# One product of the gate's seven issued behind two products of what follows, in the feed-forward part of a hybrid attention block

## The chip, the cores and the metric

The kernel runs on one core of one Trainium2 chip. The metric is the device time of one execution in microseconds (us). "Products" below are groups of matmuls on TensorE (PE); the other engines are VectorE (DVE), ScalarE (ACT), GpSimd (POOL) and the engine that issues most transfers, SyncE (SP).

## The reference

The block takes x of 2048 tokens by 1024 columns in f32. It adds to x what two kinds of attention give, and then a gated feed-forward layer:

```python
h = x
u = rms_norm(h, norm1_w)
p = u @ w_in                      # columns: diff q | k | v | sb q | k | v
yA = diff_attention(...)          # 4 heads, two softmax maps each
yB = stick_breaking_attention(...)  # 8 heads
h = h + concat(yA, yB) @ w_out
v = rms_norm(h, norm2_w)
h = h + (silu(v @ w_gate) * (v @ w_up)) @ w_down      # 2816 columns between
```

Only the last line, the feed-forward layer, is touched by the change.

## The kernel before, in words

**Precision.** Every large factor is held as two f16 parts, hi and lo, and a product of two such factors is three matmuls: hi by hi, lo by hi, hi by lo.

**Tiling.** The feed-forward layer runs in two halves of 1024 tokens. A half goes through 11 groups of 256 of the 2816 columns, so there are 22 steps, numbered 0 to 10 (first half) and 11 to 21 (second half). A step has a `gate` part and an `up` part; the `down` products of the groups are collected and done for two groups at once ("two units"), after the gates of steps 2, 4, 6, 8, 10, 11, 13, 15, 17 and 19, and once more at the end.

**Seven products.** A gate or an up is a 2 by 2 block product done with seven products in place of eight (`quad`). Each product (`product`, L1027 to L1031) is 12 matmuls of 128x512. They come in this order, each followed by its eviction from PSUM: the first, `pa` (ACT copy, L1043); `p6` (DVE add, L1047); `p7` (DVE add, L1052); `pd` (DVE add, L1057, which gives the finished block c22); a second term added into `pa`; `p4` (DVE subtract, L1067); and the seventh, which is added into the bank of `pd` (DVE add, L1071). So the seventh can't begin before L1057 has read that bank. It multiplies the seventh weight block by the token block `X[3]`. A finished block of the gate goes through SiLU on ACT (L1083, `cg` tiles). A finished block of the up is multiplied with its gate block on DVE (L1103), mixed (L98), cut into hi on ACT (L1097) and lo (L98) and kept as `act`, the input of `down`. `down` (L1131 to L1187) runs over four groups of tokens, j = 0 to 3, with seven products each (L1138); DVE accumulates them into `hs` (L1144).

**The weights' chains.** In the first half the f32 weights of the coming group are scaled and cut while the products of this group run. `load_ffn` (L921 to L1025) is a generator that does this for the gate's weights, the up's and the down's, one after the other. For each: a transfer into `stages`; a square on ACT into `sq` (L954); for gate and up a sum down the columns on PE into a bank `fsc` (L963, eight 128x256 matmuls) and its maximum on DVE (L964), for down a transposing product on PE (L183) and a maximum on DVE (L184); six or seven small DVE instructions that make the scale (L135 to L205); the mixes of blocks on POOL (L98) into `sq` and `sx`; hi parts on ACT (L216) and lo parts on DVE (L221) into the f16 tile `wg`, `wu` or `wd`; and a transfer of that tile to memory, since the second half reads it from there (L944) instead. There is one `sq`: the square of the next weights (L954) waits until the last lo part has been read out of it (L221).

**What sets the order.** The program text is a list of tiles and instructions with their dependences; a scheduler with its own estimates of durations orders each engine's instructions. Within the text the generator is advanced by hooks: `quad` calls `at(1)` to `at(7)` after its products, the last behind the seventh product, and each call issues one step of a chain. The matmuls of a chain, L963 and L183, stand inside `behind()` (L899), an order edge: they may not be placed ahead of the last matmul that `product` (or `down`'s `prod`) had issued by then, which `front[0]` remembers. It is an edge of order alone and waits for no result.

**The second half's tokens.** In steps 0 and 1 the second half's token blocks are built as well (`build_x`, L1189 to L1221, with transposes on PE, L1213, into `xtr`).

Of the kernel before, what the change touches and what calls it, by code (L numbers as in the profile page):

```python
# [16 lines left out]
ALU = mybir.AluOpType  # L17
# [23 lines left out]
CU = 3  # L41
# [18 lines left out]
def block(tc, a, out):  # L60
# [3 lines left out]
    with top:  # L64
# [64 lines left out]
        half = c1(2, "half")  # L129
# [744 lines left out]
        with ExitStack() as ph2:  # L874
# [151 lines left out]
            def product(ps_, wv, wo, X, xo, start, stop):  # L1026
                q = 0  # L1027
                for kt in range(4):
                    for xi, wi in ((0, 0), (1, 0), (0, 1)):
                        front[0] = PE.matmul(ps_[:].rearrange("p (t n) -> p t n", n=P), lhsT=wv[:, wo, wi, 128 * kt : 128 * kt + 128], rhs=X[xo][:, :, xi, kt, :], start=start and q == 0, stop=stop and q == 11, skip_group_check=not start).ins  # L1030
                        q += 1  # L1031

            def quad(wv, X, tag, bufs, c11, hooks):
                def at(n):
                    hooks(n)

                def cst():
                    return fp.tile([P, 512], F32, tag=tag, bufs=bufs, name=nm(tag))

                pa = pst("pa")  # L1040
                product(pa, wv, 0, X, 0, True, True)
                u2 = cst()
                ACT.copy(u2[:], pa[:])  # L1043
                at(1)
                p6 = pst("pm")
                product(p6, wv, 4, X, 4, True, True)
                DVE.tensor_tensor(u2[:], p6[:], u2[:], ALU.add)  # L1047
                at(2)
                p7 = pst("pm")
                product(p7, wv, 6, X, 5, True, True)  # L1050
                u3 = cst()
                DVE.tensor_tensor(u3[:], p7[:], u2[:], ALU.add)  # L1052
                at(3)
                pd = pst("pd")
                product(pd, wv, 2, X, 2, True, True)
                c22 = cst()
                DVE.tensor_tensor(c22[:], pd[:], u3[:], ALU.add)  # L1057
# [12 lines left out]
                product(pd, wv, 5, X, 3, False, True)  # L1070
                DVE.tensor_tensor(u2[:], u2[:], pd[:], ALU.add)  # L1071
                c11(0, 1, u2)
                at(7)

            def gate(W, X, hooks):
                sg = {}

                def on_gate(f, t, c):
                    if (f, t) == (0, 0):
                        s = fp.tile([P, 512], F32, tag="cg", bufs=5, name=nm("cg"))  # L1080
                    else:
                        s = c
                    ACT.activation(s[:], c[:], AF.Silu, scale=W["kg"][:])  # L1083
                    sg[f, t] = s

                quad(W["g"], X, "cg", 5, on_gate, hooks)
                note("A", 2000)
                return sg

            def up(W, X, sg, hooks, final=False):  # L1090
                if final:
                    act = stages[:].rearrange("p b n -> p (b n)").bitcast(F16)[:, :7168].rearrange("p (o s n) -> p o s n", o=7, s=2)
                else:
                    act = fp.tile([P, 7, 2, 512], F16, tag="act", bufs=2, name=nm("act"))

                def put(o, src):
                    ACT.copy(act[:, o, 0], src)  # L1097
                    note("A", 500)
                    tt(act[:, o, 1], src, act[:, o, 0], ALU.subtract, 512, LE)

                def on_up(f, t, c):
                    s = sg[f, t][:]
                    DVE.scalar_tensor_tensor(s, c[:], W["F"][:], s, op0=ALU.mult, op1=ALU.mult)  # L1103
                    if (f, t) != (0, 1):
                        put({(0, 0): 0, (1, 0): 1, (1, 1): 3}[f, t], s)
                        return
                    a11, a12, a21, a22 = (sg[k][:] for k in ((0, 0), (1, 0), (0, 1), (1, 1)))
                    s3 = fp.tile([P, 512], F32, tag="cu", bufs=CU, name=nm("cu"))
                    tt(s3[:], a11, a21, ALU.subtract, 512, SE)
                    tt(a21, a21, a22, ALU.add, 512, SE)  # L1110
                    put(2, a21)
                    tt(a11, a21, a11, ALU.subtract, 512, SE)
                    tt(a12, a12, a11, ALU.subtract, 512, SE)
                    put(6, a12)
                    put(4, a11)
                    put(5, s3[:])

                quad(W["u"], X, "cu", CU, on_up, hooks)
                note("D", 2440)
                return act  # L1120

# [6 lines left out]
                    SP.dma_start(h[q][:], hd[8 * half + 2 * j + q])  # L1128
                return h

            def down(half, units, hs, last, hook=None):  # L1131
                kd = units[-1][0]["kd"]
                nu = len(units)

                def prod(po, ao, wo, j, start=True):
                    for u, (W, act) in enumerate(units):
                        for q, (xi, wi) in enumerate(((0, 0), (0, 1), (1, 0))):
                            front[0] = PE.matmul(po[:], lhsT=act[:, ao, xi, 128 * j : 128 * j + 128], rhs=W["d"][:, wo, wi, :], start=start and u == 0 and q == 0, stop=u == nu - 1 and q == 2, skip_group_check=not start).ins  # L1138
# [12 lines left out]
                ahead = [first(j) for j in range(4)] if nu == 3 else []  # L1151
                for j in range(4):
                    if j == 2 and hook is not None:
                        hook()
                    if j + 1 < 4:
                        hs.append(load_hs(half, j + 1, nu == 3, last))
                    h0, h1 = hs[j]
                    c11, c12, c21, c22 = h0[:, :512], h0[:, 512:], h1[:, :512], h1[:, 512:]
                    note("D", 3600)
                    note("A", 500)  # L1160
                    ae = "D" if last and j == 3 else AE
                    pa = ahead.pop(0) if ahead else first(j)
                    u2 = ust()
                    ACT.mul(u2[:], pa[:], kd[:])
                    pb = pst("pd")
                    prod(pb, 4, 4, j)
                    acc(u2[:], pb, u2[:])
                    pc = pst("pd")
                    prod(pc, 5, 6, j)
                    u3 = ust()  # L1170
                    acc(u3[:], pc, u2[:])
                    tt(c12, c12, u2[:], ALU.add, 512, ae)
                    pd = pst("pd")
                    prod(pd, 2, 2, j)
                    prod(pa, 1, 1, j, False)
                    acc(c22, pd, c22)
                    prod(pd, 6, 3, j, False)
                    acc(c11, pa, c11)
                    pe = pst("pd")
                    prod(pe, 3, 5, j)  # L1180
                    acc(c12, pd, c12)
                    acc(c21, pe, c21)
                    tt(c21, c21, u3[:], ALU.add, 512, ae)
                    tt(c22, c22, u3[:], ALU.add, 512, ae)
                    for q in range(2):
                        t = 8 * half + 2 * j + q
                        SP.dma_start(out[t * P : (t + 1) * P, :] if last else hd[t], hs[j][q][:])  # L1187
# [31 lines left out]
            W = {}  # L1219
# [37 lines left out]
            for i, (half, fg) in enumerate(steps):  # L1257
# [48 lines left out]
                        go("u")  # L1306
                    row(7 + s)

                sg = gate(W, X, in_gate)
                if not more:  # L1310
                    load_now(half, fg, "d", W)
                if due:
                    down(dh, units, hs, dh != half, lambda: go("g"))
                    units = []
                act = up(W, X, sg, in_up, not more)
                if more and steps[i + 1][0] == 1:
                    go("u", 9)
                units.append((W, act))
# [27 lines left out]
```

## Time and profile before

| | |
|---|---|
| median of three runs | 2679.39 us (2678.89 to 2686.21) |
| the profiled execution's own time | 2682.59 us |
| its span in the profile | 2680.8 us |
| its mean granted TensorE clock | 0.984 |
| feed-forward part of the span, by the first and last of its instructions | about 1427 to 2681 us |
| steps 0 to 10 (first half) | about 1427 to 2060 us |

The profile's times count from the start of the span. In a row of the timeline the first number is the start of a group of like instructions, the second how long they took, then come the engine, the line of the kernel, what is written and what is read, the tile's shape, how many there were, and in brackets how long the engine was idle just before and whose end released it. In an answer on waits the three numbers are the summed idle time, how often it came, and the longest. "PEclk" is the TensorE clock that was granted, 1.00 being full speed. Step 0 begins at 1427 us, the downs of step 6 at about 1777, those of step 10 at about 2002.

### The profile page before, as it was taken

The page shows a single profiled execution, that of the slowest core. Times are in us where ns is not written, and L with a number is a line of the kernel's source. Part 1 is how long each engine was busy: PE and PEld are TensorE (multiplying, and loading weights), DVE is VectorE, ACT ScalarE, POOL GpSimd, SP SyncE. Part 2 cuts the span into 40 slices and gives each one's busy share as a digit, 9 for nine tenths or more (in the row PEclk, how much of TensorE's full clock was granted, in tenths as well). Part 3 has the DMA queues.
Part 4 walks back from the last instruction along what each step waited for, and adds up shares of the span by engine and source line. Part 5 has one row for each costly group of instructions (what it writes and reads, how often), then busy time and mean ns, then how long its engine had stood idle before and what let it go on. Part 6 is the DMA issues. An engine that isn't in the chain of part 4 may idle for free. (4 is left out here: it accounts for less than half of the span.)

```text
span 2680.8 us, 50579 instructions
## 1 busy us (share of the span) xinstructions
PE 2492.4 (93%) x19628; PEld 1498.6 (56%) x19628; DVE 1932.7 (72%) x3711; ACT 1347.0 (50%) x2487; POOL 1489.1 (56%) x1098
## 2 busy tenths in 40 slices
PE   6998989888988989889989899999999999999999
PEld 4655656577776776557775344444444444444444
DVE  6898969898989989877766868777685544444434
ACT  4665656567978878665644535344352112111121
POOL 2578667667767766546764656565564232322323
PEclk9999999999999999999999899999999999999999
DMA  6777697767998979987897574665649743635532
GB/s 222 213 162 181 146 200 168 179 143 184 193 179 179 185 160 209 210 191 217 218 285 282 208 250 178 255 226 202 245 183 346 293 177 143 233 141 186 195 111 95
DMA packets 619585, 534.41 MB, mean 199 GB/s; under 512 B 480640, under 2 KB 548224, under 8 KB 609104
## 3 DMA queue, kind: packets, MB, share of 16 engines
q1 hardware_dynamic: 617520, 529.09, 69.9%
q8 instruction: 154, 2.52, 0.4%
q0 software_dynamic: 512, 1.36, 0.2%
q14 instruction: 87, 0.71, 0.1%
q10 hardware_dynamic: 1312, 0.72, 0.1%
HBM read 261.08 MB, written 147.32 MB: 152 GB/s over the span
## 5 line engine op out<-in xcount | busy, mean ns | idle before, releaser
L98 POOL TENSOR_TENSOR s<-z,s 128x1024 f16<-128x1024 f32 (+7 forms) x288 | 472.0, 1647 | 142.5 <-ACT s L89 109.8
L507 PE MATMUL sc<-kT,qT 128*128 128x512 f16 (+3 forms) x1520 | 382.0, 353 | 53.3 <-DVE z L623 19.3
L622 DVE TENSOR_TENSOR_SCAN z<-z,sc 128x512 f32<-128x512 f32 (+3 forms) x320 | 352.8, 1112 | 58.6 <-ACT sc L620 38.0
L1138 PE MATMUL pd<-wd,act 128*128 128x512 f16 x1764 | 390.9, 379 | 1.2 <-DVE cg L1071 1.2
L326 PE MATMUL pj<-w,xt 128*128 128x384 f16 x1920 | 352.2, 331 | 18.8 <-ACT xt L683 6.9
L1030 PEld LDWEIGHTS <-wg 128*128 128x128 f16 x1848 | 182.0, 99 | 230.2 <-issue 16.4
L518 PE MATMUL yp<-v,aT 128*128 128x64 f16 (+1 forms) x4896 | 269.8, 204 | 41.6 <-DMA aT<-s 40.2
L518 PEld LDWEIGHTS <-aT 128*128 128x128 f16 x4896 | 237.5, 99 | 120.4 <-DMA aT<-s 52.5
L1030 PEld LDWEIGHTS <-wu 128*128 128x128 f16 x1848 | 180.7, 98 | 218.0 <-issue 2.6
L98 POOL TENSOR_TENSOR act<-cg,act 128x512 f16<-128x512 f32 x112 | 148.5, 1337 | 262.9 <-ACT act L1097 150.8
L1138 PEld LDWEIGHTS <-act 128*128 128x128 f16 x1764 | 172.8, 98 | 209.4 <-issue 2.8
L326 PEld LDWEIGHTS <-xt 128*128 128x128 f16 x1920 | 187.3, 99 | 147.5 <-issue 21.4
L89 ACT CAST s<-z 128x128 f16<-128x128 f32 (+7 forms) x215 | 173.1, 809 | 134.1 <-DMA aT<-s 40.5
L98 POOL TENSOR_TENSOR hs<-hs,cu 128x512 f32<-128x512 f32 x99 | 130.9, 1328 | 171.3 <-DVE hs L1144 70.8
L619 ACT ACTIVATE z<-sc,c 128x512 f32<-128x512 f32 (+3 forms) x320 | 210.7, 663 | 25.6 <-PE sc L507 11.7
L1097 ACT CAST act<-cg 128x512 f16<-128x512 f32 x126 | 77.3, 616 | 238.4 <-DVE cg L1103 162.7
L507 PEld LDWEIGHTS <-qT 128*128 128x128 f16 x1520 | 128.4, 99 | 121.0 <-DVE z L623 23.0
L832 PE MATMUL po<-wo,mt 128*128 128x256 f16 x1536 | 180.7, 277 | 13.9 <-DVE xf L835 8.4
L1030 PE MATMUL pm<-X,wu 128*128 128x512 f16 x792 | 180.4, 379 | 1.3 <-DVE wu L221 1.3
L1030 PE MATMUL pm<-X,wg 128*128 128x512 f16 x792 | 181.3, 382 | 0.0
L342 PE MATMUL pj<-xt,w 128*128 128x128 f16 x2304 | 175.0, 220 | 6.7 <-DVE v L364 5.7
L1144 DVE SCALAR_TENSOR_TENSOR hs<-pd,c,hs 128x512 f32<-128x512 f32 x136 | 99.0, 747 | 109.6 <-PE pd L1138 83.1
(266 smaller groups left out, 4737.6 us busy)
## 6 DMA issues: line engine op xcount, KB each, us to landing
xt<-xs SPq DMA_DIRECT2D x112, 512.0 KB, 4.3
hs<-hd SPq DMA_DIRECT2D x68, 512.0 KB, 4.5
hd<-hs SPq DMA_DIRECT2D x56, 512.0 KB, 4.7
split<-wg SPq DMA_DIRECT2D x11, 1792.0 KB, 7.8
split<-wu SPq DMA_DIRECT2D x11, 1792.0 KB, 6.7
split<-wd SPq DMA_DIRECT2D x11, 1792.0 KB, 7.2
wg<-split SPq DMA_DIRECT2D x11, 1792.0 KB, 7.3
wd<-split SPq DMA_DIRECT2D x11, 1792.0 KB, 12.2
```

Of the source, the lines that this page charges most:

```text
L89: ACT.copy(dst, src)
L98: (DVE if e == "D" else POOL).tensor_tensor(dst, a_, b_, op)
L326: PE.matmul(pj[:, :384], lhsT=xv[:, xi, kt, :], rhs=G["w"][:, wi, kt, :], start=n == 0, stop=n == 23)
L342: PE.matmul(o, lhsT=x_ if c == 2 else w_, rhs=w_ if c == 2 else x_, start=n == 0, stop=n == 23)
L507: last = PE.matmul(sc[:, : 128 * w].rearrange("p (t n) -> p t n", n=P), lhsT=G["q"][i // 4][:, a_, i % 4, :], rhs=G["k"][q][:, b_, 0:w, :] ...
L518: PE.matmul(yp[:, y0 : y0 + wd], lhsT=aT[:, a_, :], rhs=v[:, v_ : v_ + wd], start=start and j == 0 and q == 0, stop=stop and j == nb - 1 a ...
L619: ACT.activation(om[:, lo:hi], sc[:, :w], AF.Sigmoid, scale=G["nkz"][:])
L622: DVE.tensor_tensor_scan(ov, ov, sc[:, :w], om[:, hi : hi + 1], op0=ALU.mult, op1=ALU.bypass)
L832: PE.matmul(po[:, sl], lhsT=mt[:, kt, P * xi : P * xi + P], rhs=wos[2 * h + n][wi][:, kt, :], start=q == 0, stop=q == 23)
L1030: front[0] = PE.matmul(ps_[:].rearrange("p (t n) -> p t n", n=P), lhsT=wv[:, wo, wi, 128 * kt : 128 * kt + 128], rhs=X[xo][:, :, xi, kt, : ...
L1138: front[0] = PE.matmul(po[:], lhsT=act[:, ao, xi, 128 * j : 128 * j + 128], rhs=W["d"][:, wo, wi, :], start=start and u == 0 and q == 0, s ...
L1144: DVE.scalar_tensor_tensor(dst, po[:], kd[:], src, op0=ALU.mult, op1=ALU.add)
```

## The change

`gate` no longer issues its seventh product. `quad` puts that product, its eviction (L1071), the SiLU behind it and the last hook `at(7)` into a function `seventh`. Where a `down` follows the gate (steps 2, 4, 6, 8, 10, 11, 13, ...), it is called there for j = 0 behind the second product and its accumulation; where `up` follows, it is called behind up's second product (`p6`) and its add. The 12 matmuls of the moved product stand inside `behind()`, so they may not be placed ahead of the last matmul of that second product. Up's own seventh product stays where it was. Nothing else of the text changes; the number of matmuls, transfers and evictions is the same.

```diff
-            def quad(wv, X, tag, bufs, c11, hooks):
+            def quad(wv, X, tag, bufs, c11, hooks, before=None, late=False):
...
                 product(p6, wv, 4, X, 4, True, True)
                 DVE.tensor_tensor(u2[:], p6[:], u2[:], ALU.add)
+                if before is not None:
+                    before()
                 at(2)
...
                 at(6)
-                product(pd, wv, 5, X, 3, False, True)
-                DVE.tensor_tensor(u2[:], u2[:], pd[:], ALU.add)
-                c11(0, 1, u2)
-                at(7)
+
+                def seventh():
+                    with behind() if late else nullcontext():
+                        product(pd, wv, 5, X, 3, False, True)
+                    DVE.tensor_tensor(u2[:], u2[:], pd[:], ALU.add)
+                    c11(0, 1, u2)
+                    at(7)
+
+                if not late:
+                    seventh()
+                return seventh
...
-                quad(W["g"], X, "cg", 5, on_gate, hooks)
+                seventh = quad(W["g"], X, "cg", 5, on_gate, hooks, None, True)
...
-            def up(W, X, sg, hooks, final=False):
+            def up(W, X, sg, hooks, final=False, before=None):
...
-                quad(W["u"], X, "cu", CU, on_up, hooks)
+                quad(W["u"], X, "cu", CU, on_up, hooks, before)
...
                     acc(u2[:], pb, u2[:])
+                    if before is not None and j == 0:
+                        before()
...
-                sg = gate(W, X, in_gate)
+                sg, seventh = gate(W, X, in_gate)
...
-                    down(dh, units, hs, dh != half, lambda: go("g"))
-                    units = []
-                act = up(W, X, sg, in_up, not more)
+                    down(dh, units, hs, dh != half, lambda: go("g"), seventh)
+                    units, seventh = [], None
+                act = up(W, X, sg, in_up, not more, seventh)
```

Line numbers below L1047 shift in the changed kernel: L1057 becomes L1059, L1067 L1069, the seventh's eviction L1071 becomes L1076, L1103 becomes L1112, L1138 becomes L1147, L1213 becomes L1224.

The scheduler answers with an order that differs in more places than the edge names. Three of them follow. Tile numbers such as `_24811` are the compiler's and differ a little between the two kernels; of a product's 12 matmuls the first row stands for all.

**First place: PE in step 1**, from the end of the gate to the start of the up. `wg` is the gate's weights, `wu` the up's; `pd_22827<-X_22367` is the gate's seventh product, `fsc` the columns' sum of the next gate's weights. Before:

```order
L1030 MATMUL pm_22865<-X_22148,wg_22541 128x512
...
L1030 MATMUL pd_22827<-X_22367,wg_22541 128x512
...
L1213 MATMUL xtr_22929<-id_63,bx_22377 128x128 x4
L1030 MATMUL pm_22986<-X_21893,wu_22776 128x512
...
L963 MATMUL fsc_22900<-sq_22883,ones 128x256
...
L1030 MATMUL pa_22942<-X_21889,wu_22776 128x512
...
L1030 MATMUL pm_22966<-X_21891,wu_22776 128x512
```

In the changed kernel, same place:

```order
L1030 MATMUL pm_22865<-X_22148,wg_22543 128x512
...
L1030 MATMUL pa_22886<-X_21889,wu_22776 128x512
...
L1224 MATMUL xtr_22925<-id_63,bx_22376 128x128 x4
L1030 MATMUL pm_22986<-X_21893,wu_22776 128x512
...
L963 MATMUL fsc_22902<-sq_22883,ones 128x256
...
L1030 MATMUL pm_22943<-X_21891,wu_22776 128x512
...
L1030 MATMUL pd_22827<-X_22367,wg_22543 128x512
```

The first product of the up (`pa`) has taken the place of the gate's seventh, which now stands behind four of the up's products; the up's `p7` (`pm_22986`) and the columns' sum stay where they were.

**Second place: PE at the end of step 5's up and the gate of step 6.** `pd_24898<-X_22367` is the up's own seventh, `fsc_24917` the transposing product of the down weights' chain (L183), `pm_24948` the up's `p4`, `pd_25081<-X_22367` the gate's seventh. Before:

```order
L1030 MATMUL pa_24830<-X_22144,wu_24700 128x512
...
L183 MATMUL fsc_24917<-id_63,m_24894 128x128
L1030 MATMUL pm_24948<-X_22148,wu_24700 128x512
...
L1030 MATMUL pd_24898<-X_22367,wu_24700 128x512
...
L963 MATMUL fsc_25043<-sq_25005,ones 128x256
...
L1030 MATMUL pm_25119<-X_22148,wg_24811 128x512
...
L1030 MATMUL pd_25081<-X_22367,wg_24811 128x512
...
L1138 MATMUL pd_25184<-wd_24578,act_24497 128x512
```

In the changed kernel:

```order
L1030 MATMUL pa_24798<-X_22144,wu_24700 128x512
...
L1030 MATMUL pd_24898<-X_22367,wu_24700 128x512
...
L183 MATMUL fsc_24917<-id_63,m_24894 128x128
L1030 MATMUL pm_24948<-X_22148,wu_24700 128x512
...
L963 MATMUL fsc_25043<-sq_25005,ones 128x256
...
L1030 MATMUL pm_25119<-X_22148,wg_24813 128x512
...
L1147 MATMUL pd_25143<-wd_24578,act_24497 128x512
...
L1030 MATMUL pd_25081<-X_22367,wg_24813 128x512
```

The up's seventh has moved ahead of the down weights' L183, which now stands 16 matmuls later; the columns' sum L963 of the next weights stands behind the same number of matmuls as before; and the gate's seventh stands behind 27 matmuls of the down. The end of step 9 and the gate of step 10 show the same two moves. In the downs of steps 4 and 8 the columns' sum of the next gate's weights stands 20 and 18 matmuls earlier than before.

**Third place: DVE at the same point**, from the chain's maximum (L184) to the lo part of `wd` that is read out of `sq` (`sq_24893`), behind which the next square may begin. Before:

```order
L184 TENSOR_REDUCE m_24918<-fsc_24917 128x1
L201 TENSOR_SCALAR m_24918<-m_24918 128x1
...
L135 TENSOR_SCALAR c_24971<-c_24971,c_24533 128x1
L1067 TENSOR_TENSOR cu_24880<-cu_24880,pm_24948 128x512
L221 SCALAR_TENSOR_TENSOR wd_24916<-stages,c_24892,wd_24916 128x2x512
L1103 SCALAR_TENSOR_TENSOR cg_24731<-cu_24880,c_24534,cg_24731 128x512
L221 SCALAR_TENSOR_TENSOR wd_24916<-stages,c_24892,wd_24916 128x2x512
L221 SCALAR_TENSOR_TENSOR wd_24916<-sq_24893,c_24892,wd_24916 128x2x512
```

In the changed kernel, with most of the small instructions of the scale and two evictions left out:

```order
L184 TENSOR_REDUCE m_24918<-fsc_24917 128x1
L98 TENSOR_TENSOR cu_24989<-cg_24769,cg_24682 128x512
...
L98 TENSOR_TENSOR cg_24682<-cg_24682,cg_24752 128x512
...
L98 TENSOR_TENSOR cg_24769<-cg_24682,cg_24769 128x512
...
L135 TENSOR_SCALAR c_24971<-c_24971,c_24533 128x1
L1047 TENSOR_TENSOR cg_25024<-pm_25028,cg_25024 128x512
L98 TENSOR_TENSOR act_24797<-cg_24731,act_24797 128x512
L221 SCALAR_TENSOR_TENSOR wd_24916<-stages,c_24892,wd_24916 128x2x512
L98 TENSOR_TENSOR cg_24731<-cg_24731,cg_24769 128x512
L221 SCALAR_TENSOR_TENSOR wd_24916<-stages,c_24892,wd_24916 128x2x512
L221 SCALAR_TENSOR_TENSOR wd_24916<-sq_24893,c_24892,wd_24916 128x2x512
```

Three mixes of the up (L98) now stand between the maximum and the scale, and another L98, a lo part of `act` and the gate's L1047 between the scale and the last lo part; before, they stood behind it.

More of the change, by code (lines that the diff above doesn't have):

```diff
@@ L1084, in on_gate @@
                     sg[f, t] = s
-                quad(W["g"], X, "cg", 5, on_gate, hooks)
+                seventh = quad(W["g"], X, "cg", 5, on_gate, hooks, None, True)
                 note("A", 2000)
-                return sg
-            def up(W, X, sg, hooks, final=False):
+                return sg, seventh
+            def up(W, X, sg, hooks, final=False, before=None):
                 if final:
@@ L1129, in load_hs, with down @@
                 return h
-            def down(half, units, hs, last, hook=None):
+            def down(half, units, hs, last, hook=None, before=None):
                 kd = units[-1][0]["kd"]
```

## The prediction

> **What bounds the kernel now.** I first read the totals of the feed-forward part by stretches of time, then who keeps TensorE waiting there, then the timeline around each of those waits. Stretches; a group in brackets is the number of instructions:
>
> ```profile
> core 0: us, PE busy (x) PEld busy (x) DVE busy (x) ACT busy (x) POOL busy (x), PEclk, DMA share, GB/s
> 1427.00:2110.00 683.00, 662.54 (x3138) 309.77 (x3137) 500.93 (x749) 298.88 (x362) 379.63 (x267) 0.99 0.65 240
> 2110.00:2619.00 509.00, 509.00 (x2360) 230.72 (x2359) 212.92 (x276) 92.47 (x147) 150.42 (x119) 1.00 0.46 170
> 1469.00:1494.00 25.00, 19.53 (x89) 8.79 (x87) 24.51 (x30) 11.78 (x18) 16.60 (x12) 0.89 0.41 136
> 1494.00:1503.00 9.00, 9.00 (x52) 5.35 (x51) 2.93 (x12) 6.36 (x9) 4.71 (x4) 0.93 0.68 268
> 1503.00:1532.00 29.00, 24.38 (x114) 11.07 (x112) 27.95 (x33) 15.13 (x20) 17.57 (x10) 1.00 0.66 222
> ```
>
> In the second half (second row) PE is busy 509.00 of 509.00 us. What an order of the same matmuls can win lies in the first half, where PE idles 683.00 - 662.54 = 20.46 us. What ended those waits (summed us, how often, longest):
>
> ```profile
> PE pd L1030 <- DVE cg L1057: 8.9, 3, 5.5
> PE fsc L963 <- ACT sq L954: 5.9, 1, 5.9
> ...
> PE pm L1030 <- DVE wu L221: 1.3, 2, 0.7
> ```
>
> The first row is the wait that the change goes at: the gate's seventh product wants the bank of `pd`, and L1057 must have read it. It occurs three times in 22 gates, 8.9 us in all. The second row is the next weights' square, late for its columns' sum.
>
> **Steps 0 to 2: about -5 us.** The timeline of the waits there:
>
> ```profile
> 1443.88 2.76 PE L1030 MATMUL pd<-X,wg 128*128 128x512 f16 x12 [0.96 <-DMA X<-xcd]
> 1491.13 4.76 PE L1030 MATMUL pd<-X,wg 128*128 128x512 f16 x12 [5.47 <-DVE cg L1057]
> 1529.73 2.17 DVE L221 SCALAR_TENSOR_TENSOR wd<-sq,c,wd 128x1024 f16<-128x1024 f32 x1
> 1531.94 1.91 ACT L954 ACTIVATE sq<-stages 128x2048 bf16<-128x2048 f32 x1 [3.11 <-DVE wd L221]
> 1533.90 1.87 PE L963 MATMUL fsc<-sq,ones 128*128 128x256 bf16 x8 [5.88 <-ACT sq L954]
> 1535.56 7.34 PE L1030 MATMUL pm<-X,wg 128*128 128x512 f16 x24
> 1547.98 1.46 PE L1138 MATMUL pd<-wd,act 128*128 128x512 f16 x6 [1.19 <-DVE cg L1071]
> ```
>
> and two of DVE's own waits between 1470 and 1545 us:
>
> ```profile
> DVE cg L1052 <- PE pm L1030: 3.2, 1, 3.2
> ...
> DVE cg L1071 <- PE pd L1030: 1.2, 1, 1.2
> ```
>
> Step 0's gate waits 0.96 us for `X[3]`, the last token block to arrive; the block is needed two products later now, so this goes. In step 1 the seventh waits 5.47 us, and its 12 matmuls then take 4.76 us in place of 2.75: 2.0 us of lost clock. In the changed order the up's products stand there instead. But that up's third product reads the last lo part of `wu`, which DVE writes at about 1490, so most of the gap comes back in front of it: I count 3.4 us returned. Further back stands DVE. In the stretches above it is busy 24.51 of 25 us and 27.95 of 29, and rests only in between, at 1494 to 1503, when it has to wait for PE. So what PE wins in step 1 it waits out again in front of the columns' sum at 1533.90, except as far as DVE's rest of 9.00 - 2.93 = 6.07 us can be used. Of that rest 3.2 + 1.2 = 4.4 us are waits for PE's products, and they shrink if PE comes earlier; the remainder is not. I take the 4.4 and half of the wait of 1.19 at 1547.98: -5. Bounds: 0, if DVE's queue comes no earlier at all, and -8 (6.07, 1.19 and the 0.96 of step 0, 8.2).
>
> **Steps 4 and 8: about +1.8 us.** When `down` follows, the columns' sum inside it stands about 18 matmuls nearer to the columns' sum that its chain begins with:
>
> ```profile
> 1654.09 1.04 PE L963 MATMUL fsc<-sq,ones 128*128 128x256 bf16 x8
> 1664.74 1.91 ACT L954 ACTIVATE sq<-stages 128x2048 bf16<-128x2048 f32 x1 [1.12 <-DVE wu L221]
> 1668.99 1.04 PE L963 MATMUL fsc<-sq,ones 128*128 128x256 bf16 x8
> 1765.27 5.34 PE L1030 MATMUL pm<-X,wg 128*128 128x512 f16 x24
> 1895.84 1.91 ACT L954 ACTIVATE sq<-stages 128x2048 bf16<-128x2048 f32 x1 [1.10 <-DVE wu L221]
> 1900.29 1.04 PE L963 MATMUL fsc<-sq,ones 128*128 128x256 bf16 x8
> ```
>
> One matmul more in a sequence costs 0.216 us: 24 take 5.34 us where 12 take 2.76 (first row of steps 0 to 2), about 2.59 for each further twelve. 18 of them are 3.9 us. The square ends at 1664.74 + 1.91 = 1666.65, in step 8 at 1897.75. The covers are 1668.99 - 1666.65 = 2.3 us and 1900.29 - 1897.75 = 2.5. That leaves waits of 1.6 and 1.4; DVE's add L1071 (0.68) no longer stands ahead of the last lo part, so I take 1.1 and 0.7. Bounds: 0 and 3.
>
> **Steps 5 and 9: -0.3 us each.** In both the up's third product waits 0.66 for `wu` (1.3 in two, above). The order ahead of it is shifted by one product; the square behind it is then late by a part of the same. I take half; bounds 0 and -0.66.
>
> **Step 6: one wait goes, another comes.** Now:
>
> ```profile
> 1752.08 0.29 DVE L184 TENSOR_REDUCE m<-fsc 128x1 f32<-128x128 f32 x1
> 1758.33 1.28 DVE L221 SCALAR_TENSOR_TENSOR wd<-sq,c,wd 128x1024 f16<-128x1024 f32 x1
> 1759.64 1.91 ACT L954 ACTIVATE sq<-stages 128x2048 bf16<-128x2048 f32 x1 [1.77 <-DVE wd L221]
> 1760.79 0.69 DVE L98 TENSOR_TENSOR act<-cg,act 128x512 f16<-128x512 f32 x1
> 1761.39 0.68 DVE L1047 TENSOR_TENSOR cg<-pm,cg 128x512 f32<-128x512 f32 x1
> 1764.40 1.04 PE L963 MATMUL fsc<-sq,ones 128*128 128x256 bf16 x8
> 1764.86 3.96 DVE L98 TENSOR_TENSOR cg<-cg,cg 128x512 f32<-128x512 f32 x3
> 1773.91 4.13 PE L1030 MATMUL pd<-X,wg 128*128 128x512 f16 x12 [3.30 <-DVE cg L1057]
> 1777.84 3.10 PE L1138 MATMUL pd<-wd,act 128*128 128x512 f16 x12
> ```
>
> What goes: 3.30 us of waiting, and the slow clock behind it, 4.13 - 2.75 = 1.38 and 3.10 - 2.75 = 0.35: -5.03. The downs that stand there now read `act` parts made from the mixes that run here until 1764.86 + 3.96 = 1768.82; the new order has these mixes earlier (third place) and the new wait comes ahead of the downs, so I charge nothing for them; without that cover they would wait for the last parts.
>
> What comes: the chain of `wd` starts with L183, which the order (second place) puts 16 matmuls later, 16 x 0.216 = 3.45 us. Behind its maximum, DVE has five more instructions in front of the last lo part (third place): three mixes, an `act` lo part and L1047. Those now start 0.60 apart (1760.79 and 1761.39): 5 x 0.60 = 3.0. So the square ends 6.45 later than its 1761.55. The columns' sum stands behind the same matmuls as before and had a cover of 1764.40 - 1761.55 = 2.85. The wait is 3.6 us. If the four L98 take what the row of three shows (3.96 / 3 = 1.32 each) in place of 0.69, it is 3.6 + 4 x 0.63 = 6.1. I take 4.5, nearer the first, since the mixes would now run in front of POOL's own mixes of the next weights. A slow clock follows a wait of this length: 1.73 us behind 3.30 (above), 2.0 behind 5.47, and behind 5.88 (8 in 1.87 for 1.04, 24 in 7.34 for 5.34) 2.8. I take 2.0. New wait with its clock: 6.5, bounds 5.3 and 8.9. Step 6 in sum: +1.5.
>
> The Trainium skill, "TensorE: Matmul & The Clock Gate", section "Why this matters for your kernels", asks for no idle gaps over about 3 us between bursts, and its Part 1 gives a warm-up of about 3.4 us at half speed, by which I estimate 1.7 us lost for each such gap, whatever its length; the row at 1773.91 agrees with it (1.73), the rows at 1491.13 and 1533.90 show more (2.0 and 2.8), and by the page the sum below would be +3.6 in place of +4.2.
>
> **Step 10: +6.5 us.** The order is moved in the same two ways, but no wait of the seventh is there to go:
>
> ```profile
> 1990.06 1.28 DVE L221 SCALAR_TENSOR_TENSOR wd<-sq,c,wd 128x1024 f16<-128x1024 f32 x1
> 1991.38 1.91 ACT L954 ACTIVATE sq<-stages 128x2048 bf16<-128x2048 f32 x1 [1.78 <-DVE wd L221]
> 1996.13 1.04 PE L963 MATMUL fsc<-sq,ones 128*128 128x256 bf16 x8
> ```
>
> The cover is 1996.13 - 1993.29 = 2.84, the same as in step 6, so the same 6.5 is charged.
>
> **The second half: 0.** PE has no gap to lose. The step that hangs on the seventh there is a transfer of the next `wg`, issued on SP by the last hook. It moves back by two products, 5.2 us, and everything queued on SP behind it with it:
>
> ```profile
> 2132.33 0.32 SPq L944 DMA_DIRECT2D wg<-split  x1
> 2150.26 2.75 PE L1030 MATMUL pa<-X,wg 128*128 128x512 f16 x12
> wg<-split SPq DMA_DIRECT2D x11, 1792.0 KB, 7.3
> ```
>
> Issued at 2137.5 and landed 7.3 later at 2144.8, it is there 5.5 us before 2150.26. Were that cover gone, each of some ten steps would lose what is missing.
>
> **The sum.** -5 + 1.8 - 0.6 + 1.5 + 6.5 = +4.2 us. Against the profiled execution's own 2682.59 us this is 2686.8. That execution lies 3.2 above the median 2679.39, and a wait costs the same in either, so I put the difference on the median: 2683.6 us. A measurement of this kernel can tell about 0.3% (8 us) from no change; this is inside.
>
> **Rivals.**
>
> *Faster: the new wait doesn't come.* The mixes ahead of the scale could run while DVE would be waiting for L183 anyway, and the matmuls could be held up by the same amount elsewhere, so that the cover of 2.85 holds. For it: the idle time of DVE in these stages is large in sum (500.93 busy of 683.00). Against it: 3.45 of the delay is the order of PE's own matmuls and is above the cover by itself. Then, with no small waits in steps 4 and 8 either, -5 - 5.03 - 0.6 = -10.6: 2668.8 us.
>
> *Slower: the mixes crawl beside POOL.* In steps 6 and 10 the moved L98 collide with POOL's mixes for the next weights, so the wait is 6.1 and its clock 2.8, 8.9 in each, and in steps 0 to 2 DVE's queue gives nothing back: 0 + 1.8 - 0.6 - 5.03 + 2 x 8.9 = +14.0, 2693.4 us. It decides (over 8 us) once a new wait costs more than 5.9 with no gain in steps 0 to 2, or more than 8.4 with all 5. For it: 3.96 us for three mixes against 0.69 for one. Against it: in the row of three, what stood on POOL may not stand there any more.
>
> The Trainium skill, "GPSIMD Engine Reference", section "1. Specifications", says that GpSimd shares its SBUF interfaces with VectorE and contends with DVE instructions that have two SBUF inputs, which the mixes do; the row of three agrees in kind, and by it this rival would be the forecast.
>
> *The change doesn't act.* The first place of the order shows the seventh moved behind four products, so I give this nothing of its own.
>
> **How the numbers follow.** Forecast, around +4.2, from -3.7 (all bounds at their low end: -8 - 1.3 - 5.03 + 2 x 5.3) to +8, where the slower rival begins to decide: 0.58. Faster rival: 0.13. Slower rival: 0.29, as much as that because two steps pay for it and only one is paid back. The range 2669 to 2694 us reaches to both rivals' times; beyond them lie the outer parts of each, together under 0.2. Faster by over 0.3%: 0.13; within 0.3%: 0.58; slower by over 0.3%: 0.29.
>
> **What the changed profile would show.** The wait for L1057 by the gate's seventh (8.9 in three) is gone from the list. In its place stands L963 waiting for the square, twice with 4 to 6 us, in the gates of steps 6 and 10, and the short ones in the downs of steps 4 and 8. In step 1 the up's third product waits for `wu`. The second half is busy throughout. I am wrong if there is no wait of L963 in step 10, if DVE's five added instructions take less than 2 us, or if the gap at 1533.90 shrinks by all that step 1 wins.

## The result and the profile after

The changed kernel takes 2691.85 us (median of 14 runs, 2683.23 to 2695.43) where the kernel before takes 2682.0 (14 runs, 2677.39 to 2690.25). The ratio is 1.0032, with a 95% interval of 1.002 to 1.0043: slower by 5.4 to 11.5 us. The forecast of +4.2 us had the sign, and the range held the time, but the loss is twice the size: at 1.0032 the ratio stands just beyond the 0.3% within which the forecast had put it, on the slower rival's side, and its interval reaches to both sides of that line. These times and the ratios below are of executions with a granted clock of 0.978 or more; one execution of e8, at 0.933, is left out.

The span of the profiled execution grew from 2680.8 to 2689.2 us, +8.4. Who keeps TensorE waiting in the feed-forward part, after the change (summed us, how often, longest):

```profile
PE fsc L963 <- ACT sq L954: 21.2, 7, 7.4
PE pa L1030 <- ACT wu L216: 2.4, 1, 2.4
PE pa L1030 <- DVE wg L221: 1.9, 1, 1.9
PE pa L1030 <- DVE wu L221: 0.5, 1, 0.5
PE pm L1030 <- DVE cg L1069: 0.2, 1, 0.2
```

The wait that the change goes at, 8.9 us for the bank of `pd`, is gone altogether. The square of the next weights, which was late once, is late seven times: 5.9 us have become 21.2.

To see in which steps, one needs landmarks that stand at the same place of TensorE's order in both kernels. The transposing product of the down weights (L183) does in the ups of steps 2, 4, 6, 8 and 10, by the count of matmuls ahead of it. Before:

```profile
1594.27 0.38 PE L183 MATMUL fsc<-id,m 128*128 128x128 f32 x2
1706.99 0.38 PE L183 MATMUL fsc<-id,m 128*128 128x128 f32 x2
1825.68 0.38 PE L183 MATMUL fsc<-id,m 128*128 128x128 f32 x2
1938.72 0.38 PE L183 MATMUL fsc<-id,m 128*128 128x128 f32 x2
2051.61 0.38 PE L183 MATMUL fsc<-id,m 128*128 128x128 f32 x2
```

and after:

```profile
1590.53 0.38 PE L183 MATMUL fsc<-id,m 128*128 128x128 f32 x2
1704.27 0.38 PE L183 MATMUL fsc<-id,m 128*128 128x128 f32 x2
1825.70 0.38 PE L183 MATMUL fsc<-id,m 128*128 128x128 f32 x2
1939.01 0.38 PE L183 MATMUL fsc<-id,m 128*128 128x128 f32 x2
2059.95 0.38 PE L183 MATMUL fsc<-id,m 128*128 128x128 f32 x2
```

The differences between the two columns, step by step, are the change's effect. The first landmark, L183 at the start of step 0, stands at 1426.99 and 1427.04.

| stretch | forecast | measured |
|---|---|---|
| steps 0 to 2 | -5 | -3.8 |
| steps 3 and 4 | +1.1 | +1.0 |
| steps 5 and 6 | +1.2 | +2.7 |
| steps 7 and 8 | +0.7 | +0.3 |
| steps 9 and 10 | +6.2 | +8.0 |
| second half | 0 | +0.1 |

The new wait in step 6, on TensorE, DVE, GpSimd and ScalarE in order of time. Before, L183 stood at

```profile
1751.66 0.38 PE L183 MATMUL fsc<-id,m 128*128 128x128 f32 x2
```

and the rows of its chain are in the prediction, under step 6. After:

```profile
1751.57 0.69 DVE L1076 TENSOR_TENSOR cu<-cu,pd 128x512 f32<-128x512 f32 x1 [3.56 <-PE pd L1030]
1752.01 0.38 PE L183 MATMUL fsc<-id,m 128*128 128x128 f32 x2
1752.36 1.47 DVE L1112 SCALAR_TENSOR_TENSOR cg<-cu,c,cg 128x512 f32<-128x512 f32 x1
1753.36 1.60 POOL L98 TENSOR_TENSOR sq<-stages,sq 128x512 f32<-128x512 f32 x1
1753.75 0.28 DVE L184 TENSOR_REDUCE m<-fsc 128x1 f32<-128x128 f32 x1
1753.95 1.55 DVE L98 TENSOR_TENSOR cu<-cg,cg 128x512 f32<-128x512 f32 x1
...
1755.54 0.69 DVE L98 TENSOR_TENSOR cg<-cg,cg 128x512 f32<-128x512 f32 x1
...
1756.23 1.16 POOL L98 TENSOR_TENSOR act<-cu,act 128x512 f16<-128x512 f32 x1 [1.28 <-ACT act L1106]
1756.33 1.60 DVE L98 TENSOR_TENSOR cg<-cg,cg 128x512 f32<-128x512 f32 x1
...
1764.24 1.28 DVE L221 SCALAR_TENSOR_TENSOR wd<-sq,c,wd 128x1024 f16<-128x1024 f32 x1
...
1765.55 1.91 ACT L954 ACTIVATE sq<-stages 128x2048 bf16<-128x2048 f32 x1 [1.15 <-DVE wd L221]
...
1767.51 1.86 PE L963 MATMUL fsc<-sq,ones 128*128 128x256 bf16 x8 [6.05 <-ACT sq L954]
...
1769.17 6.17 PE L1030 MATMUL pm<-X,wg 128*128 128x512 f16 x22
```

It can be added up. TensorE reaches L183 3.4 us later, by the 16 matmuls that stand ahead of it (the two times of L183, 1751.66 and 1752.01, nearly agree since the stretch begins 2.7 us earlier after the change and step 5's wait is 0.4 shorter). From L183 to the maximum L184 it takes 1753.75 - 1752.01 = 1.74 us, since DVE first evicts and multiplies the up's seventh (L1076, L1112); before it was 1752.08 - 1751.66 = 0.42: +1.3. From L184 to the end of the last lo part read out of `sq` it takes 1765.52 - 1753.75 = 11.8 us, before 7.5: +4.2. In sum 9.0, less the cover of 2.85: 6.1, and 6.05 was measured. The slow clock behind it: 8 in 1.86 us for 1.04, and 22 matmuls in 6.17 for 22 x 0.216 + 0.16 = 4.91: 2.1 us. In step 10 the wait is the same:

```profile
2002.26 1.86 PE L963 MATMUL fsc<-sq,ones 128*128 128x256 bf16 x8 [6.04 <-ACT sq L954]
```

### The profile page after: what moved, and what is told of

Same layout as the page of the kernel before. It is cut to its first block, busy times and chain, and to the rows that moved or that the text cites. A ratio compares the mean times of both kernels' runs of the same rounds, so it can differ in the third digit from the quotient of the medians.

```text
span 2689.2 us, 50596 instructions
## 1 busy us (share of the span) xinstructions
PE 2495.4 (93%) x19628; PEld 1498.8 (56%) x19628; DVE 1926.8 (72%) x3711; ACT 1345.3 (50%) x2487; POOL 1483.6 (55%) x1098
## 5 line engine op out<-in xcount | busy, mean ns | idle before, releaser
L98 POOL TENSOR_TENSOR s<-z,s 128x1024 f16<-128x1024 f32 (+7 forms) x288 | 471.3, 1645 | 139.6 <-ACT s L89 114.5
L1147 PE MATMUL pd<-wd,act 128*128 128x512 f16 x1764 | 391.0, 379 | 0.0
L98 POOL TENSOR_TENSOR act<-cg,act 128x512 f16<-128x512 f32 x112 | 152.6, 1374 | 276.7 <-ACT act L1106 164.6
L1147 PEld LDWEIGHTS <-act 128*128 128x128 f16 x1764 | 172.5, 98 | 207.4
L98 POOL TENSOR_TENSOR hs<-hs,cu 128x512 f32<-128x512 f32 x99 | 128.1, 1298 | 173.8 <-DVE hs L1153 84.0
```

Of the source, the lines that this page charges most:

```text
L98: (DVE if e == "D" else POOL).tensor_tensor(dst, a_, b_, op)
```

## The experiments

In the table, each kernel's feed-forward stretches in the profile, between the same landmarks, in us; the last column is from the end of step 10 to the end of the span. What lies ahead of step 0 differs by up to 10 us from one profile to another (L183 of step 0 stands at 1418.8 to 1428.6 us), and this view leaves that out. Ratios are those of the runs against the kernel before on the same chip.

| kernel | 0 to 2 | 3, 4 | 5, 6 | 7, 8 | 9, 10 | rest | ratio, 95% interval |
|---|---|---|---|---|---|---|---|
| before | 167.3 | 112.7 | 118.7 | 113.0 | 112.9 | 629.2 | |
| after | 163.5 | 113.7 | 121.4 | 113.3 | 120.9 | 629.3 | 1.0032, 1.002 to 1.0043 |
| e1 only 5 and 9 | 167.4 | 112.7 | 122.5 | 113.0 | 120.9 | 629.2 | 1.0053, 1.004 to 1.0067 |
| e2 all but 5 and 9 | 163.5 | 113.8 | 114.0 | 113.3 | 112.9 | 629.2 | 0.9974, 0.9964 to 0.9984 |
| e3 mixes behind | 163.5 | 113.8 | 116.1 | 113.3 | 114.8 | 629.6 | 0.9984, 0.9975 to 0.9994 |
| e4 up's seventh in place | 157.6 | 114.1 | 115.9 | 113.3 | 113.9 | 629.6 | 0.9959, 0.9946 to 0.9972 |
| e5 steps 0, 1, 2, 6, tied | 157.8 | 112.7 | 115.1 | 113.0 | 112.9 | 629.4 | 0.9942, 0.9929 to 0.9954 |
| e6 steps 0, 1, 2, 6 | 163.8 | 112.7 | 114.0 | 113.1 | 112.9 | 629.5 | 0.9959, 0.9946 to 0.9971 |
| e7 second half alone | 167.5 | 112.7 | 118.5 | 113.1 | 112.9 | 629.2 | 0.9991, 0.9981 to 1.0002 |
| e8 weights' step early | 165.0 | 114.4 | 125.6 | 116.8 | 123.3 | 629.4 | 1.0077, 1.0059 to 1.0096 |
| e9 GpSimd, one input | 163.6 | 115.4 | 119.5 | 113.3 | 117.9 | 629.2 | 1.001, 0.9991 to 1.003 |
| e10 no edge | 162.6 | 113.1 | 113.5 | 113.3 | 112.3 | 629.2 | 0.9954, 0.9939 to 0.9969 |

Theory A, after the result: the late seventh wins where DVE was late, but in steps 5 and 9 it lets the scheduler put the up's own seventh ahead of L183 on TensorE and the mixes ahead of the scale on DVE, and the down weights' chain then ends too late for the next square. Rival B: what costs in steps 6 and 10 is their own seventh with its weights' step, moved behind products of the down.

**e1 and e2: the change in steps 5 and 9 alone, and everywhere else.** `gate` gets a flag; where it is off, the seventh is issued in its old place.

```diff
-                sg, seventh = gate(W, X, in_gate)
+                sg, seventh = gate(W, X, in_gate, i in (5, 9))      # e1
+                sg, seventh = gate(W, X, in_gate, i not in (5, 9))  # e2
```

> Only the gates of steps 5 and 9 issue their seventh product late; all other steps as before. Theory A (the late seventh of these two gates lets the scheduler put the up's own seventh ahead of the down weights' transposing product, and the mixes ahead of the scale, so the next square is late): the columns' sum waits about 6 us for the square in the gates of steps 6 and 10, with some 2 us of slow clock behind each; the wait of 3.30 us in step 6 goes; in sum +10 to +13 us against before. Rival B (the loss in steps 6 and 10 comes from their own seventh products and the weights' steps moved behind the downs): no such waits, 0 us.

> The change in every step but 5 and 9. Theory A: no wait for the square in steps 6 and 10; steps 0 to 2 keep -3.8 us, step 4 +1.0, step 6 loses its wait of 3.30 and the slow clock, -5.0, step 8 +0.3; in sum about -7.5 us against before. Rival B: the two waits of 6 us stay, about +8 us.

e1 is slower by a ratio of 1.0053 (+14 us; +12.0 in the profile). Steps 6 and 10 show the two waits, although their own sevenths stand as before:

```profile
1770.37 1.86 PE L963 MATMUL fsc<-sq,ones 128*128 128x256 bf16 x8 [6.05 <-ACT sq L954]
...
2005.96 1.86 PE L963 MATMUL fsc<-sq,ones 128*128 128x256 bf16 x8 [6.05 <-ACT sq L954]
```

e2 is faster, 0.9974; the profile gives -7.2 us for the -7.5 that were expected, and neither wait is there. Rival B falls: the loss of steps 6 and 10 is made in steps 5 and 9, and e2's steps 5 and 6 take 114.0 us for 118.7, a gain of 4.7 where 5.0 was expected of the late seventh in step 6.

**e3: TensorE's order or DVE's?** In steps 5 and 9 an order edge holds the up's first mixes behind the last lo part; TensorE's order stays as changed up to the gate's end. `lo_part` holds the latest lo part that was issued (L221).

```diff
-                    tt(s3[:], a11, a21, ALU.subtract, 512, SE)
-                    tt(a21, a21, a22, ALU.add, 512, SE)
+                    with tc.issue_after(lo_part[0]) if hold else nullcontext():
+                        tt(s3[:], a11, a21, ALU.subtract, 512, SE)
+                        tt(a21, a21, a22, ALU.add, 512, SE)
```

> The change in every step, and in steps 5 and 9 an order edge that keeps the up's four mixes on DVE behind the last lo part of the down weights; TensorE's order is that of the change up to the gate's end, with the transposing product 16 matmuls later than before. If DVE's added instructions and TensorE's order both make the wait: 3.4 (16 matmuls) + 1.3 (two evictions that DVE has ahead of the maximum) + 0.6 (the gate's add) - 2.85 of cover = 2.5 us in each of steps 6 and 10, little slow clock, about -2 us against before. If the place of the transposing product alone decides: 6 us of wait as in the change, +8. If the mixes alone decide: no wait, about -7.

The waits in steps 6 and 10:

```profile
1754.91 1.03 PE L965 MATMUL fsc<-sq,ones 128*128 128x256 bf16 x8 [1.65 <-ACT sq L956]
...
1984.33 1.03 PE L965 MATMUL fsc<-sq,ones 128*128 128x256 bf16 x8 [1.65 <-ACT sq L956]
```

1.65 us of 6.05 are left, and no slow clock follows (8 in 1.03). Of the 2.5 expected, 0.85 is missing: in this kernel it takes 7.4 us from L184 to the end of the lo part, less than before, although the gate's add stands in between. So 1.65 us come of TensorE's order with the two evictions, and 4.4 of DVE's mixes and the lo part of `act` that follows them. Both are needed to make 6. The whole feed-forward part is 2.7 us shorter than before, where 2 were expected.

**e4: the up's seventh held behind its p4**, in every step, by the same kind of edge as the change's.

```diff
-                    with behind() if late else nullcontext():
+                    with behind():
                         product(pd, wv, 5, X, 3, False, True)
```

> The change in every step, and the up's own seventh product stands inside an order edge as well, so that it can't pass its p4. The transposing product of steps 5 and 9 then stands 10 matmuls (2.2 us) later than before in place of 16, and DVE's order from the maximum to the last lo part is that of before. Theory A: the cover of 2.85 us holds, no wait for the square in steps 6 and 10, about -7 us against before. If the place of the transposing product alone decides: waits of 6.05 - 1.3 = 4.75 us in both, about +5.

```profile
1521.39 1.03 PE L963 MATMUL fsc<-sq,ones 128*128 128x256 bf16 x8 [1.91 <-ACT sq L954]
...
1750.55 1.03 PE L963 MATMUL fsc<-sq,ones 128*128 128x256 bf16 x8 [1.21 <-ACT sq L954]
```

0.9959, and -9.5 us in the profile. In step 6 (second row) and in step 10 the wait is 1.2 us, between the two expectations but far nearer to A. DVE's order is not quite that of before: the eviction of the up's seventh and the lo part from `sx` now stand ahead of the last one from `sq`, and L184 to its end takes 9.5 us for 7.5. The 10 matmuls (2.2 us) alone would have stayed within the cover of 2.85. What had not been expected stands in the first row. In step 2 the wait is 1.91 us where the change has 7.44 and the kernel before 5.88, and steps 0 to 2 take 157.6 us, 9.7 less than before, where the change wins 3.8. There, too, the up's seventh had passed L183 in the change (in step 1, where L183 stands 24 matmuls later than before), with mixes between the maximum and the scale.

**e5 and e6: steps 0, 1, 2 and 6 alone, with and without that edge in step 1.**

```diff
-                sg, seventh = gate(W, X, in_gate)
+                sg, seventh = gate(W, X, in_gate, i in (0, 1, 2, 6))
...
-                    with behind() if late else nullcontext():
+                    with behind() if late or tied else nullcontext():   # e5: tied in the up of step 1
```

> Late seventh in the gates of steps 0, 1, 2 and 6 alone, and in step 1 the up's own seventh held behind its p4 by an order edge. Theory A (what the late seventh wins is undone wherever the up's seventh passes the down weights' transposing product, in step 1 as in 5 and 9): steps 0 to 2 about -9.7 us as in the run with all the ups' sevenths held, step 6 about -4.7, the rest as before: -14 us against before. If steps 0 to 2 are bound by DVE's amount of work, as the prediction had it: -3.8 - 4.7 = -8.5.

> Late seventh in the gates of steps 0, 1, 2 and 6 alone, no other edge. Both theories: steps 0 to 2 about -3.8 us as in the change, with the wait of 7 us for the square in step 2, step 6 about -4.7, the rest as before: -8.5 us against before.

e6 has the wait of 7.4 us in step 2, e5 has 1.91:

```profile
1529.15 1.87 PE L963 MATMUL fsc<-sq,ones 128*128 128x256 bf16 x8 [7.43 <-ACT sq L954]
```

```profile
1524.28 1.03 PE L963 MATMUL fsc<-sq,ones 128*128 128x256 bf16 x8 [1.91 <-ACT sq L954]
```

The two differ by 6.0 us in steps 0 to 2 (163.8 and 157.8), for one edge; in steps 5 and 6 e5 takes 1.1 us more, and in all e6 gains 7.9 us where 8.5 were expected. e5 has the lowest ratio of this study, 0.9942 (0.9929 to 0.9954), though the intervals of e4, e6 and e10 overlap it, and -13 us in the profile's feed-forward part; -14 was expected. The 8.5 that a bound by DVE's amount of work would allow is passed.

**e7: the second half alone.**

```diff
-                sg, seventh = gate(W, X, in_gate)
+                sg, seventh = gate(W, X, in_gate, half == 1)
```

> Late seventh in the gates of steps 11 to 21 alone. Theory A: the feed-forward part takes the same time as before to 0.3 us, since the transfer of the next gate's weights keeps 5 us of cover; 0 us. Rival (the transfers issued later on SP are missed somewhere): a wait of the gate's or the up's first product for a transfer, up to 5 us in each of ten steps.

Nothing moves: 0.9991 (0.9981 to 1.0002), and the stretch that answers to the second row of the prediction's windows reads

```profile
2107.00:2616.00 509.00, 509.00 (x2360) 230.79 (x2359) 213.62 (x276) 92.33 (x147) 150.58 (x119) 1.00 0.46 169
```

**e8: only the product moves, the weights' step stays.**

```diff
                     c11(0, 1, u2)
-                    at(7)
 
                 if not late:
                     seventh()
+                at(7)
```

> The change in every step, but the weights' step stays at the gate's end; only the product moves. The columns' sums of steps 3, 5, 7 and 9 then stand 12 matmuls (2.6 us) nearer to the chain's beginning than in the change, with covers of 1.0, 0.4, 0.1 and 0.4 us in the profile before: new waits of 1.6, 2.2, 2.5 and 2.2 us, about +8 on top of the change's own +8.4, so +16 against before. If the moved weights' step is what costs: less than the change, about 0.

1.0077, and +20.6 us in the profile. The four covers were read rightly; the waits in steps 3, 5, 7 and 9:

```profile
1621.31 1.03 PE L963 MATMUL fsc<-sq,ones 128*128 128x256 bf16 x8 [1.47 <-ACT sq L954]
...
1737.05 1.03 PE L963 MATMUL fsc<-sq,ones 128*128 128x256 bf16 x8 [2.04 <-ACT sq L954]
...
1861.99 1.25 PE L963 MATMUL fsc<-sq,ones 128*128 128x256 bf16 x8 [2.24 <-ACT sq L954]
...
1979.43 1.03 PE L963 MATMUL fsc<-sq,ones 128*128 128x256 bf16 x8 [2.04 <-ACT sq L954]
```

for 1.6, 2.2, 2.5 and 2.2 expected. The weights' step has to go with the product, since the columns' sum is placed by it. The other 4 us or so lie in three places. Behind the wait in step 7 the granted clock was 0.74 from 1864 to 1868 us, and 12 matmuls took 4.27 us where 2.75 is usual:

```profile
1863.03 4.27 PE L1030 MATMUL pm<-X,wu 128*128 128x512 f16 x12
```

In step 6 the late seventh waits 1.26 us for L1059, and steps 0 to 2 take 1.5 us more than in the change, with a wait of 10.07 us for the square in step 1.

**e9: why the mixes are long.** In the ups of steps 5 and 9 GpSimd copies one tile in place of adding or subtracting two; the orders of the other engines are those of the change.

```diff
-            (DVE if e == "D" else POOL).tensor_tensor(dst, a_, b_, op)
+            if e == "P" and single[0]:
+                POOL.tensor_scalar(dst, b_, 1.0, 0.0, op0=ALU.mult, op1=ALU.add)
+            else:
+                (DVE if e == "D" else POOL).tensor_tensor(dst, a_, b_, op)
```

> The change in every step; during the ups of steps 5 and 9 each of GpSimd's subtractions and additions (mixes of the weights, lo parts of act) is replaced by a copy of its second input, so GpSimd reads one tile of SBUF in place of two; the values are wrong there, and the orders of TensorE and DVE are those of the change. If the three mixes on DVE are long (1.55, 0.69 and 1.60 us in the change, for 0.69 alone) because GpSimd reads two tiles at once with them: all three near 0.7, the wait for the square in steps 6 and 10 about 4.3 in place of 6.05 us, some 4 us less in sum than the change. If they are long for another reason: 6.05 as in the change.

```profile
1749.38 0.68 DVE L103 TENSOR_TENSOR cu<-cg,cg 128x512 f32<-128x512 f32 x1
1750.10 0.69 DVE L103 TENSOR_TENSOR cg<-cg,cg 128x512 f32<-128x512 f32 x1
1750.89 1.05 DVE L103 TENSOR_TENSOR cg<-cg,cg 128x512 f32<-128x512 f32 x1
```

```profile
1750.80 1.63 POOL L101 TENSOR_SCALAR act<-act 128x512 f16<-128x512 f16 x2 [3.49 <-ACT act L1111]
...
1761.85 1.86 PE L968 MATMUL fsc<-sq,ones 128*128 128x256 bf16 x8 [4.23 <-ACT sq L959]
```

The mixes take 0.68, 0.69 and 1.05 us for 1.55, 0.69 and 1.60, and the wait is 4.23 us for 6.05 (4.24 in step 10), with 4.3 expected. So 1.8 us of the wait are DVE beside GpSimd's additions: 1.1 behind the maximum, and 0.7 ahead of it, where the multiplication L1112 took 1.47 us and takes 0.75 here. That GpSimd reads one tile in place of two is not what these rows show, though the expectation put it so. The copies are short, 0.62 us each, so that GpSimd stood idle from 1747.31 to 1750.80, while the first two mixes ran; the third began beside a copy of one tile and took 1.05. The time of the whole stretch is 3.2 us under the change's, 4 were expected. Steps 3 and 4 take 1.7 us more here, behind waits for the downs' sums that this edit doesn't explain.

**e10: without the edge.** The text is that of the change, the product may be drawn forward.

```diff
-                    with behind() if late else nullcontext():
+                    if True:
                         product(pd, wv, 5, X, 3, False, True)
```

> The seventh product and its weights' step stand in the text where the change has them, but without the order edge, so the scheduler may draw the product forward; the transposing product of steps 5 and 9 then stands 4 matmuls later than before in place of 16, with the up's seventh split around it and DVE's mixes behind the chain. Theory A: 0.9 us of TensorE's order and 0.7 of one more add stay within the cover of 2.85, no wait for the square in steps 6 and 10; step 6 wins 4.7, steps 0 to 2 win 4 to 8 (the seventh of step 1 stands near its old place and may wait for DVE again); about -8 us against before. If the late place in the text alone costs: +8.

0.9954 (0.9939 to 0.9969), and -9.9 us in the profile: neither of the two waits in steps 6 and 10, 5.2 us won in steps 5 and 6, 4.7 in steps 0 to 2, where the wait in step 2 is still 7.06 us. The scheduler, left free, splits the up's seventh around L183. So the late place in the text isn't what costs. With the edge on the gate's seventh the scheduler draws the up's seventh ahead of L183, and without it, or with a second edge on the up's (e4), it doesn't.

## Why the prediction was right, and what it had wrong

- **The waits for `pd` go: right.** All 8.9 us went, and the new waits stand where the forecast put them, at the columns' sums in the gates of steps 6 and 10.
- **The new wait in steps 6 and 10: right in mechanism, too small.** The term was 4.5 us, between 3.6 and 6.1; measured 6.05 and 6.04. The step that was mis-sized is the stretch between L183 and the maximum: the working counted only what stands behind the maximum and put this at nothing, while the two evictions there cost 1.3 us by the rows of step 6. What stands behind the maximum was nearly right: 4.5 allows 3.9 us for it, and 4.2 was measured. It was right in part by chance, since the working counted five added instructions where the third place of the order has six, and since the mixes did run beside GpSimd (1.55 and 1.60 us), which the choice of 4.5 had spoken against. The slower rival's 6.1 is the measured wait by luck: it charged 5.5 us behind the maximum and nothing ahead of it. Its other condition, that steps 0 to 2 give nothing back, did not hold. e9 shows that GpSimd does make a part of the wait, 1.8 us. The Trainium skill, "GPSIMD Engine Reference", section "1. Specifications", names this contention of DVE instructions with two SBUF inputs, and here the runs agree with it: a mix took 1.55 to 1.60 us beside GpSimd's additions and 0.69 without. The slow clock, taken at 2.0, was 2.1 in step 6 and 2.5 in step 10. Steps 5 and 6 came out 1.5 us over the forecast, 9 and 10 by 1.8: 3.3 of the 4.2 us that it falls short.
- **Steps 0 to 2: -5 forecast, -3.8 measured, and the reason was wrong, so that the near number is luck.** The step that failed reads that what PE wins in step 1 it waits out again "except as far as DVE's rest of 9.00 - 2.93 = 6.07 us can be used". It took DVE's amount of work for the bound. The gap at 1533.90 did grow, from 5.88 to 7.44 us, but e5 against e6 shows that it is the same thing as in steps 5 and 9: in step 1, too, the up's seventh passed L183. In e5, with the same work on DVE, the gap is 1.91 us. With that undone the stretch wins 9.5 us, beyond the -8 that had been the bound. The order of step 1 had been read only up to the columns' sum of the gate's weights, and the down weights' chain behind it was not looked for.
- **The up's third product as the place where the gap returns: wrong in place.** It is the up's first that waits in step 1, 2.97 us where 3.4 were counted, and 2.1 us of slow clock are lost there as well (10 matmuls in 4.45 us, where 2.33 is usual), which the working did not charge:

```profile
1485.14 1.04 PE L1030 MATMUL pa<-X,wu 128*128 128x512 f16 x2 [2.42 <-ACT wu L216]
1486.73 4.45 PE L1030 MATMUL pa<-X,wu 128*128 128x512 f16 x10 [0.55 <-DVE wu L221]
```

- **Steps 4 and 8: right in kind, a little too large.** 1.1 and 0.7 us were expected; measured 0.86 and 0.19:

```profile
1661.95 1.03 PE L963 MATMUL fsc<-sq,ones 128*128 128x256 bf16 x8 [0.86 <-ACT sq L954]
...
1896.70 1.03 PE L963 MATMUL fsc<-sq,ones 128*128 128x256 bf16 x8 [0.19 <-ACT sq L954]
```

- **Steps 5 and 9: right.** 0.66 us for `wu` became 0.30 for the square, -0.36 each where -0.3 was taken.
- **The second half: right**, by e7 and by the last column of the table.

## What to carry to other kernels

An order edge on one product also orders, through the scheduler, the products next to it; what it costs is looked for at every other chain that passes the same place, here the next weights', and on both engines, the one that starts the chain and the one that works it off. Before a moved instruction is priced, list what now stands between a chain's start and the instruction that ends it, what stands ahead of the start included, and compare with that chain's cover. Where the waits of a change fall in a few steps only, apply it in those steps: the change in four of 22 steps and one more edge makes a gain of 0.6% of what was a loss of 0.3%.

## What the runs showed of the hardware

- A DVE addition of two 128x512 f32 tiles took 0.68 to 0.69 us when no GpSimd instruction was running as it began. When one was, it took what was left of that instruction and 0.55 us more: in the rows of step 6 above, 1.55 us with 1.01 left, 1.60 with 1.06 left, and 0.69 in the gap between the two. In the feed-forward part of the changed kernel 46 of 48 such additions fit this to 0.01 us; the two others took 0.68 to 0.69. Beside the copy of one tile in e9 it was the same, 1.05 us with 0.52 left.
- The slow clock behind a wait of TensorE doesn't follow from its length alone. The wait of 3.30 us in step 6 cost 1.73 us more before; the same wait in e7 was followed by 12 matmuls at full clock, and the down's second product then waited 1.26 us for DVE, so that steps 5 and 6 took about the same (118.5 and 118.7):

```profile
1770.95 2.75 PE L1030 MATMUL pd<-X,wg 128*128 128x512 f16 x12 [3.30 <-DVE cg L1059]
...
1776.25 1.46 PE L1148 MATMUL pd<-wd,act 128*128 128x512 f16 x6 [1.26 <-DVE cg L1076]
```

- The eight matmuls of a columns' sum alone don't show the slow clock. In e8 they took 1.03 us behind a wait of 2.04 us, and the next 12 matmuls 2.75; behind the wait of 2.24 us they took 1.25, and the next 12 took 4.27. Behind the wait of 4.24 us in step 10 of e9 they took 1.14 us, and the next 24 took 6.97, where 5.34 is usual.
